# A hybrid decoder layer: the output projection of two token tiles at a time by one level of Strassen, and a re-paced second filter

## The chip, the cores and the metric

The kernel runs on one core of a Trainium2 chip. The core has five engines with their own instruction queues: TensorE (PE, matmuls), VectorE (DVE), ScalarE (ACT), GpSimd (POOL) and SyncE (SP, which here issues most DMAs). They share an on-chip memory (SBUF), in which the kernel's buffers lie; matmuls write to banks of a second memory (PSUM). The metric is the device time of one execution in microseconds, and the result of a version is the median of its runs.

## The reference

One decoder layer over 2048 tokens of width 1024, in float32, cut to what matters here:

```
hn     = rms_norm(h, mix_pre_g)
proj   = hn @ w_in                                  # q, k, v and the convolution's input u
attn   = sliding_window_attention(q, k, v, ...)     # window 128, 512 channels
conv   = conformer_conv(u, ...)                     # gate, 31-tap filter, LayerNorm, silu, pointwise; 512 channels
mixed  = concatenate([attn, conv]) @ w_out          # 1024 -> 1024: the output projection
h      = h + rms_norm(mixed, mix_post_g)
hn     = rms_norm(h, ffn_pre_g)
ff     = (silu(hn @ w_gate) * (hn @ w_up)) @ w_down # 1024 -> 2816 -> 1024
h      = h + rms_norm(ff, ffn_post_g)
```

Float32 products are made of three products each: both factors are split into a high part (a rounded copy) and a low part (the rest), and high·high, high·low and low·high are summed in PSUM (`three`, L167).

## The kernel before

**Tiles and stages.** The 2048 tokens are four tiles of 512. Letters name the stages, digits the tiles; in the profile a buffer's stage stands behind the "@". A is the input projection (`stage_a`), B the attention, whose result goes to rows 0 to 3 of a DRAM buffer `mixT`. T0 and T1 (`stage_taps`, L534) are the 31-tap filter of tile pairs 0/1 and 2/3: four channel groups of 50 VectorE operations each, shown under the label C. C (`stage_tail`, L586) is the rest of the convolution, LayerNorm and the pointwise product in the PSUM bank `ct`, and writes rows 4 to 7 of `mixT`. W (`stage_w`, L712) is the output projection; `norm_w` (L751) does what follows it for a tile: sum of squares, reciprocal root, scaling by `mix_post_g`, adding x, storing h, a second sum and root, and the scaled tile `hn`, which goes to `hn_scr` as well.

The FFN works on tile pairs and already uses one level of Strassen: H (`stage_h_plain` L833, `stage_h_sums` L846) reads `hn_scr` back, turns it on PE and makes plain operands and operand sums; F (`stage_pre` L891, then `stage_p1` L961) is the gate and up products; G (`stage_p2` L1119) the down product. H0, F0, G0 belong to tiles 0 and 1, H2, F2, G2 to tiles 2 and 3. `stage_pre` does those products of F that need plain operands only (20 matrices, two halves each of 12 matmuls, before the first p1, whose first product is the first to read a sum).

**The projection before.** `stage_w` works on one tile: eight chunks of 128 input channels, in groups of G = 2. `acts` loads a chunk of `mixT` into the raw buffer `mtag` and splits it (ScalarE the high part at L723, VectorE the low part); `weight` (L119) loads two weight chunks, and `split_w` (L108) makes the high part on ScalarE and the low part on POOL or, with `made`, loads a low part that an earlier tile left in `lo_out`. `block_half` (L686) does four token blocks of one half of the output columns: matmuls into a PSUM bank, then a copy (ScalarE, first group) or an addition (VectorE) into the tile's accumulator. That is 4 groups x 2 halves x 4 blocks x 6 matmuls = 192 a tile, 384 a pair.

**Order of the work.** Main work is a generator that `run` steps through; each step gives its cost, and by that cost lanes of side work earn credit (`Lane`, L1277) at a rate of their own: `lb` attention, `lc` filters, `lw` projections, `ld` tails, `lf`, `lh` FFN operands, `lt`. A lane's item may have a condition; `until` runs a lane through to a named item. The instructions then go to in-order queues, one an engine, in an order that a scheduler makes of it.

- W0 is an item of `lw`, once A3 has started and C0 is done. `lw.until("W0")` after A3 finishes it, its norm included; the H0 operands of tile 0 (B11.0, B21.0) become items of `lh`.
- W1 is main work, and with `ready` the first Q0 = 8 products of F0 run in its middle; its norm is given to `lh`. The sums S0 wait for product 22 of F0, B3 and T1.
- C2, W2, C3, W3 are items of `lw` beside G0 (`run(stage_p2((0, 1), ...))`), then N3 and B11.2; after G0, `lw.until("N3")` ends them, and F2 is main work.
- Raw chunks of W2 and W3, and the x that `norm_w` adds, use the tag `at`, of which there are two buffers.

Of the kernel before, what the change touches and what calls it, by code (L numbers as in the profile page):

```python
# [12 lines left out]
F32 = mybir.dt.float32  # L13
# [26 lines left out]
def layer_kernel(ctx, tc, x, xT, cols, rows, sinks, relb, onehot, w_in, w_pw, w_out, w_gate, w_up, w_down, out):  # L40
# [14 lines left out]
    BUFS = dict(x=4, p=4, wx=1, gb=2, hl=8, ql=4, chl=5, mid=4, mb=2, fa=4, at=2, fc=3, glu=1, yt=1, raw=2, w=6)  # L55
# [63 lines left out]
    def weight(src, low, made, raw=None, on_pool=True):  # L119
        if raw is None:  # L120
            raw = t_("raw", (P, 2, T))
            nc.sync.dma_start(raw, src)
        return [split_w(raw[:, n], "w", low[n], made, on_pool) for n in range(2)]
# [52 lines left out]
    lo_out = dr.tile([2, KC, P, T], F32, name="lo_out")  # L176
# [46 lines left out]
    kz = cst.tile([P, 2, P + T], F32R, name="kz")  # L223
    nc.gpsimd.memset(kz[:, :, 0:P].bitcast(F32), 0.0)
    junk = cst.tile([P, D], F8, name="junk")
    vtok = cst.tile([P, 5, P], F32, name="vtok")
# [307 lines left out]
    def stage_taps(p):  # L534
# [7 lines left out]
        for c in range(4):  # L542
# [14 lines left out]
            ay = t_("mb", (P, 2, T))  # L557
# [25 lines left out]
            nc.sync.dma_start(y_scr[c, :, p, 1], a)  # L583
            yield 0.0
# [101 lines left out]
    def block_half(acc, units, n, first, L, bank_of, s0=0):  # L686
        cs = slice(n * T, (n + 1) * T)
        for i in range(len(acc)):
            s = i + s0
            lab[0] = L  # L690
            o = bank_of()
            three(o, [((a[s // 4][:, 0, ss(s)], a[s // 4][:, 1, ss(s)]), (w[:, 0], w[:, 1])) for a, w in units])
            if first:
                act(acc[i][:, cs], o, AF.Copy)  # L694
            else:
                vtt(acc[i][:, cs], acc[i][:, cs], o, ALU.add)
            yield 0.65 * len(units)

# [13 lines left out]
    def stage_w(w, spill, G, atag, htag, mtag, bank_of, norm=None, ready=None):  # L712
        L = f"W{w}"
        lab[0] = L
        acc = [f4(atag) for _ in range(4)]

        def acts(gi):
            aa = []
            for c in range(G * gi, G * gi + G):
                m = f2(mtag)  # L720
                nc.sync.dma_start(m, mixT[c, :, w * T : (w + 1) * T])
                a = hl(htag)
                act(a[:, 0], m, AF.Copy)  # L723
                vtt(a[:, 1], m, a[:, 0].bitcast(F32), ALU.subtract)
                aa.append([a])
            return aa

        nxt = acts(0)
        for gi in range(KC // G):
            aa = nxt  # L730
            for n in range(2):
                lab[0] = L
                if n == 1 and gi + 1 < KC // G and not (ready and G * gi + G == 4):
                    nxt = acts(gi + 1)
                ws = weight(w_out[2 * gi : 2 * gi + 2, :, n * T : (n + 1) * T].rearrange("c p t -> p c t"),
                            lo_out[n, 2 * gi : 2 * gi + 2], w > 0)
                yield from block_half(acc, list(zip(aa, ws)), n, gi == 0, L, bank_of)
            if ready and G * gi + G == 4:
                for i, c in enumerate(ready()):
                    if i == Q0 // 2:  # L740
                        ld.until("C1")
                        lab[0] = L
                        nxt = acts(gi + 1)
                    yield c
        tail = norm_w(w, spill, acc, mtag)
        if norm:
            norm(tail)
        else:
            yield from tail

    def norm_w(w, spill, acc, mtag):  # L751
# [33 lines left out]
        for s in range(4):  # L785
            act(acc[s], acc[s], AF.Copy, scale=r2[:, s : s + 1])
            if spill:
                r0 = w * T + s * P
                nc.scalar.dma_start(hn_scr[r0 : r0 + P], acc[s])
# [291 lines left out]
    def stage_tsums(td):  # L1081
        L = "G0"
        for pr in range(NF // 2):
            lab[0] = L
            wx = f4("wx", (P, 2, T))
            b = [wx[:, 0], wx[:, 1], f2("fc"), f2("fc")]
# [235 lines left out]
    RC0, RC1, RW0, RW, RB, LC = 1.1, 0.9, 1.7, 1.25, 0.8, 100  # L1322
# [11 lines left out]
    Q0 = 8  # L1334
# [6 lines left out]
    lw = Lane(RW0, 0)  # L1341
# [4 lines left out]
    lanes = [lb, lc, lw, ld, lf, lh, lt]  # L1346
    lh.rates = {"N1": 1.2, "S0": 0.9, "H0": 1.2}
    lc.rates = {"T0": RC0, "T1": RC1}
    lw.rates = {"W0": RW0, "C2": RW, "W2": RW, "C3": RW, "W3": RW}
# [13 lines left out]
    lw.add("W0", stage_w(0, True, 2, "x", "hl", "fa", mm), lambda: "A3" in started and "C0" in ld.done)  # L1363
# [6 lines left out]
    for p in range(2):  # L1370
        lc.add(f"T{p}", stage_taps(p))
    for t in range(2):
        ld.add(f"C{t}", stage_tail(t), lambda: since(lc, "T0", CS))
    for t in range(NT):
# [33 lines left out]
    lw.until("W0")  # L1408
# [5 lines left out]
    for n, off in (("B11", 0), ("B21", 4)):  # L1414
        lh.add(n + ".0", stage_h_plain(ws, ops, n, off))
    run(stage_w(1, True, 2, "mid", "hl", "at", mm, norm=lambda g: lh.add("N1", g), ready=lambda: stage_pre(ws, ops, mids[0], keeps[0], 0, Q0)))
    lh.until("B21.0")
    lh.add("S0", stage_h_sums(ws, ops), lambda: f"P0.{PRE_S0}" in started and "B3" in lb.done and "T1" in lc.done)
    run(stage_pre(ws, ops, mids[0], keeps[0], Q0))
# [5 lines left out]
    lw.add("W2", stage_w(2, True, 2, "mid", "ql", "at", tr))  # L1425
# [74 lines left out]
```

## Time and profile before

| | us |
|---|---|
| median of 3 runs | 2112.7 |
| lowest and highest run | 2109.73 and 2113.94 |
| the profiled execution, its own time | 2107.25 |
| its span in the trace | 2105.5 |
| PE busy in the span | 1980.8 |
| VectorE busy in the span | 1448.8 |

The span runs from the first to the last recorded instruction; the rest of the execution's time lies around it. In the rows below, a group is a source line, an engine, an operation and "out<-in" with buffer names and stage letters, then partitions x elements, the count, busy microseconds, the mean of one in nanoseconds, and the idle time of the engine before them with what ended it. A timeline row gives the start in microseconds, the duration (of the whole run, where "x8" says that eight stand together), and in brackets the idle time before it with what ended it. A row of the DMA view ends with the size of one transfer and the median of the microseconds from issue to landing.

### The profile page before, as it was taken

How to read it: one execution, taken by the hardware profiler on the slowest of the kernel's cores; microseconds unless marked ns; L12 is line 12 of the kernel's file. 1: busy time of each engine (PE TensorE's matmuls, PEld its weight loads, DVE VectorE, ACT ScalarE, POOL GpSimd, SP SyncE). 2: the span in 40 equal slices, each digit the busy share in tenths (PEclk: the TensorE clock that was granted, in tenths of full speed). 3: DMA queues.
4: the chain of work that ended last, by engine and by line, in shares of the span. 5: the costliest groups of instructions: out<-in, count | busy, mean ns of one | idle time of the engine just before them, and what ended most of it. 6: DMA issues, size and time to landing. Idle time of an engine off the chain costs nothing. (4 is left out here: it accounts for less than half of the span.)

```text
span 2105.5 us, 27138 instructions
## 1 busy us (share of the span) xinstructions
PE 1980.8 (94%) x8826; PEld 1578.7 (75%) x8826; DVE 1448.8 (69%) x2530; ACT 990.4 (47%) x1938; POOL 410.7 (20%) x467
## 2 busy tenths in 40 slices
PE   9999997789797889999999999989999999999997
PEld 7777775467575667788877878878788888888886
DVE  4578999967799877767645465468476666446557
ACT  5455454436644653334336457356553343335443
POOL 4011022333311310000001103105333333220003
PEclk9999999799899999999999999999999999999999
DMA  8776645357665999854447678677964443266654
GB/s 312 259 267 225 206 160 166 119 167 257 221 196 186 331 319 310 278 170 168 147 155 245 212 227 292 209 258 265 338 212 167 170 166 124 91 220 228 194 191 148
DMA packets 237086, 451.32 MB, mean 214 GB/s; under 512 B 23400, under 2 KB 53264, under 8 KB 236944
## 3 DMA queue, kind: packets, MB, share of 16 engines
q1 hardware_dynamic: 216400, 419.18, 59.2%
q10 hardware_dynamic: 20544, 30.42, 3.9%
q8 instruction: 69, 1.13, 0.2%
q14 instruction: 73, 0.60, 0.1%
HBM read 330.48 MB, written 119.02 MB: 213 GB/s over the span
## 5 line engine op out<-in xcount | busy, mean ns | idle before, releaser
L888 PE MATMUL mm@F<-hl@H,w@F 128*128 128x512 f32 x1056 | 257.8, 395 | 9.4 <-ACT mm@F L928 9.4
L1158 PE MATMUL mm@G<-hl@G,hl@G 128*128 128x512 f32 x924 | 232.8, 399 | 10.8 <-ACT hl@G L801 4.6
L888 PEld LDWEIGHTS mm@F<-hl@H,w@F 128*128 128x128 f32 x1056 | 200.5, 191 | 53.6 <-ACT mm@F L928 11.7
L801 ACT ACTIVATE w@F<-chl@F 128x512 fp32r<-128x512 f32 x220 | 135.6, 625 | 166.1 <-PE mm@F L888 159.4
L1158 PEld LDWEIGHTS mm@G<-hl@G,hl@G 128*128 128x128 f32 x924 | 173.8, 191 | 51.2 <-ACT hl@G L801 5.4
L172 PE MATMUL mm@A<-hl@A,w@A 128*128 128x512 f32 x840 | 205.1, 395 | 5.2 <-DVE ql@A L87 2.1
L1158 PE MATMUL mm@G<-w@G,hl@G 128*128 128x512 f32 x876 | 199.4, 389 | 0.0
L1158 PEld LDWEIGHTS mm@G<-w@G,hl@G 128*128 128x128 f32 x876 | 164.4, 188 | 34.1
L87 DVE TENSOR_TENSOR w@F<-chl@F,w@F 128x512 fp32r<-128x512 f32 x198 | 146.2, 739 | 58.6 <-ACT w@F L801 58.1
L172 PEld LDWEIGHTS mm@A<-hl@A,w@A 128*128 128x128 f32 x840 | 154.9, 188 | 41.5 <-DVE ql@A L87 2.3
L888 PE MATMUL mm@F<-ql@H,w@F 128*128 128x512 f32 x528 | 131.5, 396 | 7.5 <-ACT mm@F L1035 4.7
L888 PE MATMUL mm@F<-x@H,w@F 128*128 128x512 f32 x528 | 127.6, 395 | 9.8 <-ACT fa@F L950 9.8
L888 PE MATMUL mm@F<-p@H,w@F 128*128 128x512 f32 x528 | 131.8, 395 | 0.0
L888 PE MATMUL mm@F<-mid@H,w@F 128*128 128x512 f32 x528 | 129.9, 392 | 1.8 <-DVE at@F L87 1.4
L888 PEld LDWEIGHTS mm@F<-x@H,w@F 128*128 128x128 f32 x528 | 100.2, 191 | 31.4 <-ACT fa@F L950 10.2
L888 PEld LDWEIGHTS mm@F<-ql@H,w@F 128*128 128x128 f32 x528 | 99.8, 190 | 31.2 <-ACT mm@F L1035 5.7
L112 ACT ACTIVATE w@A<-raw@A 128x512 fp32r<-128x512 f32 x110 | 67.6, 627 | 109.3 <-PE mm@A L172 75.7
L888 PEld LDWEIGHTS mm@F<-p@H,w@F 128*128 128x128 f32 x528 | 101.1, 192 | 21.6 <-ACT at@F L1049 0.2
L888 PEld LDWEIGHTS mm@F<-mid@H,w@F 128*128 128x128 f32 x528 | 98.5, 188 | 23.7 <-DVE at@F L87 1.8
L172 PE MATMUL mm@W<-w@W,hl@W 128*128 128x512 f32 x384 | 103.9, 418 | 10.6 <-ACT x@W L694 4.9
L87 DVE SCALAR_TENSOR_TENSOR mb@C<-wx@C,dws,mb@C 128x512 f32<-128x512 f32 x128 | 106.2, 830 | 1.8
L172 PE MATMUL tr@W<-w@W,ql@W 128*128 128x512 f32 x384 | 99.4, 397 | 6.7 <-ACT mid@W L694 4.8
(303 smaller groups left out, 3612.0 us busy)
## 6 DMA issues: line engine op xcount, KB each, us to landing
mids<-fa@F SPq DMA_DIRECT2D x154, 256.0 KB, 2.4
raw@A<-w_in SPq DMA_DIRECT2D x55, 512.0 KB, 4.4
w@A<-lo_in SPq DMA_DIRECT2D x84, 256.0 KB, 3.3
fc@G<-mids SPq DMA_DIRECT2D x77, 256.0 KB, 3.4
fa@G<-mids SPq DMA_DIRECT2D x75, 256.0 KB, 4.6
gb@F<-keeps SPq DMA_DIRECT2D x72, 256.0 KB, 4.3
raw@W<-w_out SPq DMA_DIRECT2D x32, 512.0 KB, 5.1
w@W<-lo_out SPq DMA_DIRECT2D x48, 256.0 KB, 3.5
```

What stands on the lines that cost most here:

```text
L87: r = op(*args, **kw)
L112: act(w[:, 0], raw, AF.Copy)
L172: mat(o, a, b, start=first and i == 0, stop=last and i == n - 1)
L801: act(w[:, 0], x, AF.Copy)
L888: mat(o, w[:, a, ks], op[k][:, b], start=first and n == 0, stop=n == 11, skip_group_check=not first)
L1158: mat(banks[b], p_, q_, start=start and z == 0, stop=stop and z == 2, skip_group_check=True)
```

## The change

`stage_w` now takes a pair of tiles and forms the product by seven half-size products (types 0 to 6) in place of eight. Type by type it does 4 token blocks of 12 matmuls: 7 x 4 x 12 = 336 a pair. Types 0 and 1 use tile one's channels 0 to 3 and 4 to 7 as they are, type 6 tile two's 4 to 7; types 2 to 5 use sums of the four. The first tile's accumulator is complete after type 4, the second's after type 6, and each is then handed with its norm to `on_tile`.

- `stage_wsums` (TW, lane `ld`, once A1 has started) makes four differences of weight quarters on POOL, 16 subtractions, into the DRAM buffer `tw`. `stage_wacts` (SA, lane `ld`) loads both tiles' `mixT` chunk by chunk, makes the four operand sums with 16 VectorE operations a pair, and stores them to `sa`, from where `acts` loads them.
- For the first pair `deep` loads and splits the next type's operands during the present one, and POOL makes all 28 low weight parts and leaves them in `lo_out`; the second pair loads them, and fetches a type's operands only after the type before.
- The first pair is main work after A3: `ld.until("SA")`, then `run(stage_w((0, 1), ...))`. N0, B11.0 and B21.0 go to `lh` after type 4, N1 after type 6. The eight products of F0 that ran inside W1 go back to the rest of F0 (Q0 is gone).
- S0 waits for "y11" (the second of T1's four channel groups stored) in place of the whole T1.
- Second pair in `lw`: C2, C3, SA2, W2; N2 goes to `lf`, N3 to `lw`, B11.2 waits for N2; `lw.until("W2")` after G0.
- Rates: filters RC0 1.1 to 1.4 and RC1 0.9 to 0.6; attention of tile 3 gets 0.55; W's 1.25 only.
- Buffers: T1's groups from the third on use `kz` in place of `mb`, and `stage_tsums` uses `vt` in place of `wx`, both former constants of their own.

```diff
-    lo_out = dr.tile([2, KC, P, T], F32, name="lo_out")
+    lo_out = dr.tile([7, 4, P, T], F32, name="lo_out")
+    tw = dr.tile([4, 4, P, T], F32, name="tw")
+    sa = [dr.tile([4, 4, P, T], F32, name=f"sa{i}") for i in range(2)]
...
-            ay = t_("mb", (P, 2, T))
+            ay = t_("kz" if p and c > 1 else "mb", (P, 2, T))
...
             nc.sync.dma_start(y_scr[c, :, p, 1], a)
+            started.add(f"y{p}{c}")
...
+    def stage_wsums():
+        for c in range(4):
+            y = t_("yt", (P, 4, T))
+            for i in range(4):
+                k, n = c + 4 * (i // 2), i % 2
+                nc.sync.dma_start(y[:, i], w_out[k, :, n * T : (n + 1) * T])
...
+            for to, o, p_, q_ in ((0, b11, b12, b11), (2, b12, b22, b12), (1, b22, b22, b11), (3, b21, b21, b22)):
+                ptt(o, p_, q_, ALU.subtract)
+                nc.sync.dma_start(tw[to, c], o)
...
+    def stage_wacts(ws):
+        for c in range(4):
+            r = [t_("chl", (P, 2, T)) for _ in range(2)]
...
+            vtt(s12[:, 0], r[1][:, 0], r[1][:, 1], ALU.add)
+            vtt(s12[:, 1], s12[:, 0], r[0][:, 0], ALU.subtract)
+            vtt(s34[:, 0], r[0][:, 0], r[1][:, 0], ALU.subtract)
+            vtt(s34[:, 1], r[0][:, 1], s12[:, 1], ALU.subtract)
+            nc.sync.dma_start(sc[0:2, c].rearrange("j p t -> p j t"), s12)
+            nc.sync.dma_start(sc[2:4, c].rearrange("j p t -> p j t"), s34)
...
+    def stage_w(ws, tags, htag, mtag, bank_of, deep, made, on_tile):
...
+        def evict(ty, b, o):
+            h = [x and (x[b][:, 0:T], x[b][:, T:]) for x in acc]
+            if ty == 0:
+                act(h[0][1], o, AF.Copy)
+            elif ty == 1:
+                vtt(h[0][0], h[0][1], o, ALU.add)
+            elif ty == 2:
+                vtt(h[1][0], h[0][1], o, ALU.add)
+            elif ty == 3:
+                act(h[1][1], o, AF.Copy)
+                vtt(h[0][1], h[1][0], o, ALU.add)
+            elif ty == 4:
+                vtt(h[0][1], h[0][1], o, ALU.add)
+            elif ty == 5:
+                vtt(h[1][0], h[1][0], o, ALU.add)
+                vtt(h[1][1], h[1][1], h[1][0], ALU.add)
+            else:
+                vtt(h[1][0], h[1][0], o, ALU.add)
...
+        aa, wt = acts(0, range(4)), weights(0, 0) + weights(0, 1)
+        for ty in range(7):
...
+            for b in range(4):
+                if deep and ty < 6:
+                    if b == 0:
+                        na += acts(ty + 1, (0, 1))
...
+                o = bank_of()
+                three(o, [((a[:, 0, ss(b)], a[:, 1, ss(b)]), (w[:, 0], w[:, 1])) for a, w in zip(aa, wt)])
+                evict(ty, b, o)
+                yield 2.72
...
+            if ty == 4:
+                on_tile(ws[0], norm_w(ws[0], acc[0], mtag))
+        on_tile(ws[1], norm_w(ws[1], acc[1], mtag))
...
-    RC0, RC1, RW0, RW, RB, LC = 1.1, 0.9, 1.7, 1.25, 0.8, 100
+    RC0, RC1, RW, RB, LC = 1.4, 0.6, 1.25, 0.8, 100
...
+    lb.rates = {"B3": 0.55}
...
-    lw.add("W0", stage_w(0, True, 2, "x", "hl", "fa", mm), lambda: "A3" in started and "C0" in ld.done)
...
+    ld.add("TW", stage_wsums(), lambda: "A1" in started)
...
+    ld.add("SA", stage_wacts((0, 1)), lambda: "B1" in lb.done)
...
-    run(stage_w(1, True, 2, "mid", "hl", "at", mm, norm=lambda g: lh.add("N1", g), ready=lambda: stage_pre(ws, ops, mids[0], keeps[0], 0, Q0)))
+    def on_first(w, norm):
+        lh.add(f"N{w}", norm)
+        if w == 0:
+            for n, off in (("B11", 0), ("B21", 4)):
+                lh.add(n + ".0", stage_h_plain(ws, ops, n, off))
+    ld.until("SA")
+    run(stage_w(ws, ("x", "mid"), "hl", "fa", mm, True, False, on_first))
...
-    lw.add("W2", stage_w(2, True, 2, "mid", "ql", "at", tr))
     lw.add("C3", stage_tail(3))
-    lw.add("W3", stage_w(3, True, 2, "mid", "ql", "at", tr, norm=lambda g: lw.add("N3", g)))
-    lw.add("B11.2", stage_h_plain(ws, ops, "B11", 0))
+    lw.add("SA2", stage_wacts(ws))
+    lw.add("W2", stage_w(ws, ("mid", "chl"), "ql", "at", tr, False, True, lambda w, norm: (lf if w == 2 else lw).add(f"N{w}", norm)))
+    lw.add("B11.2", stage_h_plain(ws, ops, "B11", 0), lambda: "N2" in lf.done)
     run(stage_p2((0, 1), mids[0], td))
+    lw.until("W2")
     lw.until("N3")
```

126 lines of the change are left out of this document (65 added, 61 removed).

## The prediction

> **What bounds the kernel now.** I read the page's totals first, then busy time by stretches cut at the places where TensorE (PE) passes from stage to stage, then the costs by group, and last the timeline around both places where the output projection (W) runs. The stretches:
>
> ```profile
> span 2105.5 us, 27138 instructions
> PE 1980.8 (94%) x8826; PEld 1578.7 (75%) x8826; DVE 1448.8 (69%) x2530; ACT 990.4 (47%) x1938; POOL 410.7 (20%) x467
> ...
> 0.00:200.00 200.00, 193.51 (x912) 150.97 (x912) 129.30 (x299) 100.79 (x217) 35.74 (x59) 1.00 0.76 268
> 200.00:420.00 220.00, 192.09 (x931) 140.25 (x929) 212.88 (x453) 97.80 (x260) 52.04 (x58) 0.93 0.52 166
> 420.00:525.00 105.00, 97.99 (x402) 71.47 (x403) 74.28 (x105) 50.49 (x87) 36.28 (x45) 0.92 0.63 210
> 525.00:775.00 250.00, 206.91 (x915) 157.72 (x914) 209.41 (x386) 132.30 (x272) 57.21 (x69) 0.92 0.74 251
> 775.00:1103.00 328.00, 319.25 (x1388) 261.62 (x1387) 217.50 (x344) 123.17 (x219) 0.00 (x0) 0.99 0.61 206
> 1103.00:1456.00 353.00, 337.18 (x1498) 274.27 (x1497) 209.15 (x357) 201.27 (x362) 60.82 (x96) 0.98 0.74 247
> 1456.00:2106.00 650.00, 633.90 (x2793) 522.46 (x2791) 396.25 (x589) 284.63 (x523) 168.64 (x141) 0.99 0.55 187
> ```
>
> After window and length the columns are busy time (and count) of PE, PEld, VectorE, ScalarE and POOL, then granted clock, DMA share, GB/s. PE bounds the whole at 94%, but not evenly. In the first 775 us it is busy 690.5 (the four rows added) and idle 84.5, with VectorE at 213 of 220 us in the second row. The last three rows have only 8.8, 15.8 and 16.1 us of PE idle. So removed matmuls are worth their full price after 775 us if nothing new stops PE; before 775 the filters and chains on VectorE decide.
>
> ```profile
> 1600.00:1650.00 50.00, 50.00 (x222) 41.42 (x221) 33.48 (x42) 19.26 (x35) 17.72 (x12) 1.00 0.51 173
> ...
> L172 PE MATMUL mm@W<-w@W,hl@W 128*128 128x512 f32 x384 | 103.9, 418 | 10.6 <-ACT x@W L694 4.9 <-ACT hl@W L723 4.3 <-DVE mid@W L87 1.3
> L172 PE MATMUL tr@W<-w@W,ql@W 128*128 128x512 f32 x384 | 99.4, 397 | 6.7 <-ACT mid@W L694 4.8 <-ACT ql@W L723 1.9
> ```
>
> An undisturbed stretch passes 222 matmuls in 50 us: **0.225 us each**. W is 384 matmuls for each pair of tiles (mm@W the first, tr@W the second), 203.3 us busy in all, with 17.3 us of waits of its own.
>
> **What is removed.** Seven products of four blocks of 12 matmuls are 336 a pair instead of 384: 48 x 0.225 = **-10.8 us per pair**, -21.6 in all. That is the most that the change can take out of PE. The stages not touched (p1 in the window from 775, and from 1456 to the end) I carry over at 327.5 and 649.
>
> **First part, up to p1.** Here W0 ran beside the last input projection, its norm and the H0 operands were ready while W1 ran, and PE had something to do meanwhile:
>
> ```profile
> 358.38 3.12 DVE L87 SCALAR_TENSOR_TENSOR mb@C<-wx@C,dws,mb@C 128x512 f32<-128x512 f32 x4
> 459.55 0.63 ACT L640 ACTIVATE fc@C<-ct@C 128x512 f32<-128x512 f32 x1 [1.63 <-PE ct@C L172]
> 466.21 0.60 ACT L527 ACTIVATE yt@C<-ct@C 128x512 f32<-128x512 f32 x1 [0.59 <-PE ct@C L526]
> 489.45 1.28 DVE L87 TENSOR_TENSOR x@W<-x@W,mm@W 128x512 f32<-128x512 f32 x2 [2.70 <-PE mm@W L172]
> 510.79 2.33 PE L172 MATMUL mm@A<-hl@A,w@A 128*128 128x512 f32 x9
> 541.72 1.13 ACT L786 ACTIVATE x@W<-x@W,sm@W 128x1024 f32<-128x1024 f32 x1
> 550.66 1.03 PE L819 MATMUL tr@H<-ident,fa@H 128*128 128x128 f32 x8
> 554.51 1.15 ACT L842 ACTIVATE x@H<-gb@H 128x512 fp32r<-128x512 f32 x2 [0.31 <-ACT chl@C L112]
> 572.43 0.64 ACT L640 ACTIVATE fc@C<-ct@C 128x512 f32<-128x512 f32 x1 [0.40 <-ACT gb@H L839]
> 587.73 2.88 PE L888 MATMUL mm@F<-x@H,w@F 128*128 128x512 f32 x12
> 775.16 1.52 PE L888 MATMUL mm@F<-mid@H,w@F 128*128 128x512 f32 x6
> ```
>
> The first filter pair ends at 361.5. The first tail (C0) ends at 460.2, 98.7 us later; C1 takes 466.2 to 573.1, 107 us. From W0's last addition (490.7) the norm runs to 542.9 (52 us), the transposes begin 7.8 us later, and the first operands are there at 555.7: **65 us from a tile's last addition to its first FFN operand.** W1 and the tails covered that.
>
> In the order of the changed program A3's last matmul is PE instruction 1,848 (2,097 before). The first two rows of the stretches count 1,843 PE instructions by 420 us, so A3 ends near **416** instead of 513. Only 72 W matmuls stand ahead of the second tail's work: products from the third on read the sums of mixT that the new SA pass makes out of both tails, and PE's next 175 instructions are only B3 and C1. Without W0 beside them I take 80 us for each tail, below the 98.7 and 107 shown: 361.5 + 160 = 521.5, and 18 us for the SA pass (four chunks, each loaded, added, stored and loaded again at 4.4 us a transfer, row below): W resumes near **540**. Bounds: 490 with tails of 60 us, 572 if C1 ends as it does now.
>
> From there 264 W matmuls remain, 59 us. The fifth product completes tile 0 after 168 of them: 540 + 38 = 578. Then the 65 us: 643. Products six and seven cover 21.6 us and PE runs out near 600, so some **35 us of idle appear** (less some B3 work). F0 begins near 642. Its 480 matmuls ahead of p1 cost 108 us at 0.225, and 137 at the rate of the stretch that holds them now:
>
> ```profile
> 700.00:750.00 50.00, 39.94 (x175) 32.37 (x176) 44.27 (x62) 33.61 (x61) 16.12 (x12) 0.93 0.98 336
> ...
> 750.28 1.75 DVE L87 TENSOR_TENSOR ql@H<-chl@H,ql@H 128x512 fp32r<-128x512 f32 x1
> ```
>
> That is 50/175 = 0.286 with the DMA engines at 0.98. The loads stay and the projection adds some, so I take 130, nearer the upper end: p1 begins near **772**, against 775, **-3**.
>
> A second path gives the same. p1 needs the operand sums, whose last operation ends at 752.0 on a VectorE that is busy 625.9 us up to 775. Ahead of that operation the changed order still has 198 of T1's 200 filter operations (200 before); the new gate on "y11" lets them start earlier, but the queue is no shorter. The pair itself has 72 VectorE operations in place of 64 (28 evictions, 28 splits, 16 sums against 48 and 16), +8 x 0.684. "Second filter spread" thus moves work and removes none: it takes cover from the first half and gives it to the second. If VectorE's idle time there falls by a third, 40 us, p1 begins at 740 (-35); if W resumes at 572 it begins near 800 (+25). These are the bounds.
>
> ```profile
> L87 DVE TENSOR_TENSOR mid@W<-mid@W,tr@W 128x512 f32<-128x512 f32 x48 | 32.1, 684 | 25.2 <-PE tr@W L172 25.2
> L114 POOL TENSOR_TENSOR w@W<-raw@W,w@W 128x512 fp32r<-128x512 f32 x16 | 23.1, 1447 | 66.1 <-ACT w@W L112 56.8 <-DMA raw@W<-w_out 9.2
> L87 DVE SCALAR_TENSOR_TENSOR x@W<-x@W,sm@W,gb@W 128x512 f32<-128x512 f32 x8 | 7.4, 997 | 1.2 <-POOL sm@W L141 1.2
> L87 DVE SCALAR_TENSOR_TENSOR mid@W<-mid@W,sm@W,gb@W 128x512 f32<-128x512 f32 x24 | 16.2, 745 | 8.8 <-DMA gb@W<-rows 5.0 <-POOL sm@W L141 3.8
> ```
>
> POOL gets 16 subtractions of weight quarters and 28 low parts instead of 16: 28 x 1.447 = 40.5 us. It is busy 181 of the first 775 us, so I cost this at nothing; uncovered, the 28 low parts alone pace W at 40.5 us against its 76 of matmuls, which still fits. The row x@W shows the same VectorE operation at 997 ns, mid@W at 745, with two SBUF inputs each. The Trainium skill (SBUF — State Buffer, "Who interferes with whom") says that a VectorE operation with two SBUF inputs and a POOL operation that reads SBUF hold one port pair in turn, each for its whole length, which speaks against giving POOL more work. By it the 28 additions could cost VectorE up to 40 us and p1 would begin later by as much; by the two rows, 252 ns a collision, 7 us. No run here separates the two yet.
>
> **Second part, beside G0.** Now tile 2's projection and norm end in the middle of G0, and tile 3's follow:
>
> ```profile
> 1233.19 1.52 PE L172 MATMUL tr@W<-w@W,ql@W 128*128 128x512 f32 x6
> 1234.75 0.69 DVE L87 TENSOR_TENSOR mid@W<-mid@W,tr@W 128x512 f32<-128x512 f32 x1 [0.90 <-PE tr@W L172]
> ...
> 1242.66 5.39 DVE L87 SCALAR_TENSOR_TENSOR mid@W<-mid@W,sm@W,gb@W 128x512 f32<-128x512 f32 x8 [2.32 <-POOL sm@W L141]
> ...
> 1257.61 0.69 DVE L87 TENSOR_TENSOR mid@W<-at@W,mid@W 128x512 f32<-128x512 f32 x1 [3.60 <-DMA at@W<-x]
> ...
> 1268.42 0.68 DVE L87 TENSOR_TENSOR mid@W<-at@W,mid@W 128x512 f32<-128x512 f32 x1
> ...
> 1282.93 1.13 ACT L786 ACTIVATE mid@W<-mid@W,sm@W 128x1024 f32<-128x1024 f32 x1
> ...
> 1452.66 2.49 PE L1158 MATMUL mm@G<-hl@G,hl@G 128*128 128x512 f32 x9 [0.49 <-DVE hl@G L87]
> 1456.22 5.96 PE L888 MATMUL mm@F<-ql@H,w@F 128*128 128x512 f32 x25
> ...
> at@W<-mixT SPq DMA_DIRECT2D x24, 256.0 KB, 4.4
> at@W<-x SPq DMA_DIRECT2D x14, 256.0 KB, 5.7
> ```
>
> The norm takes 1235.4 to 1284.1, **48.6 us**, all behind G0's matmuls; F2's first product starts 1.1 us after G0's last one ends (1455.2). In the changed order G0's last matmul comes first, and **144 W2 matmuls (products five to seven) and 20 transposes of H2 follow it with nothing of G0 between.** The fifth product completes tile 2, so its norm now starts after G0 has run out. On PE only products six and seven, 96 x 0.225 = 21.6 us, stand beside it.
>
> The seventh is late too. Its raw operands use the two "at" buffers and stand on SyncE's queue behind the norm's residual loads; ScalarE's split of its fourth chunk stands behind the norm's four scalings. So, counted from tile 2's last addition: scalings done at 48.6; the last split and its low part about 1.3; the rest of product seven 10.5; then the transposes (1.0 a row of four blocks) and copies and splits to the first operand 4 to 5: **F2 begins about 65 us after product five**, with 22 to 23 us of PE work in it: 42 us idle. If the gaps between residual additions (1251.6 to 1268.4, waiting for x) vanish, the norm takes 34 and the idle is 27.
>
> Stage from 1103 to 1456: 353.5 - 10.8 + 42, and +3 for product five, whose operands come one load and split after product four without prefetch, less 8 of its 15.8 us idle, as W's chunk waits (6.7, row tr@W) go with G0 work at hand: 379.7. I take the middle of 42 and 27 nearer the row as measured, 40: **+24**. Bounds +5 (norm of 34, all present idle gone) and +35 (nothing of it gone, seventh product fully behind).
>
> **The sum** against the profiled execution's own 2107.25 (span 2105.5 and 1.75 around it): -3 + 0 + 24 + 0 = +21, and 2128. The median shown, 2112.7, lies 5.5 above that execution; on its footing the forecast is 2112.7 + 21 = 2134, and I say **2132**.
>
> The row 420 to 525 grants 0.92 of the clock, the busy stretch at 1600 all of it. The Trainium skill (TensorE: Matmul & The Clock Gate, "Why this matters for your kernels") has the clock fall to half after about 3 us without matmuls, and a like time of work to restore it. By it the two new gaps would cost some 1.7 us each beyond their length, +3.4, as an estimate; the sum above leaves it out.
>
> **The rivals.**
> 1. *The gaps are covered* (faster). Norms of 34 us as bounded above, F0 drawn forward because VectorE is freed of W0 beside A3, and PE's 21.6 us come through: first part -25, second 0: 2088. For it: 17.5 us of the 48.6 are waits for x at a time when G0 shares every engine, and G0 will be gone. Against it: products six and seven put their loads, evictions and splits into the same queues, in the same two buffers.
> 2. *No net change.* One gap of about half my size and the saving cancel: 2112. Nothing in the profile prefers exactly this.
> 3. *The tails decide* (much slower). SA makes W wait for C1. If both tails run on VectorE beside T1 at today's 98.7 and 107 us, W resumes at 572, p1 begins at 800, and with +24 behind G0 the time is 2112.7 + 25 + 24 = 2162. It decides once C1 ends past 550. For it: both tails go through one PSUM bank, in line, and T1 and B3 share VectorE with them. Against it: W0's work left that stretch.
> 4. *The change does not do what it says*: the filter is not spread where it counts. That is already in my forecast (198 of 200).
>
> **How the numbers follow.** Forecast 0.45, with its own range 2116 to 2150; rival 1 0.28; rival 2 0.10; rival 3 0.17. What a measurement can tell from no change is about 4 us. Faster has rival 1, 0.28; same most of rival 2, 0.09; slower the rest, 0.63. The range 2092 to 2168 takes in rival 3 and rival 1's upper half.
>
> **What would show it.** PE without matmuls for over 30 us between W's seventh product and F0's first, and again between G0's last matmul and F2's first product: then both gap terms hold. C1's last row near 520 and W's resumption near 540 test the third number; p1's first product near 772 the first sum. I am wrong if F2 starts within 35 us of product five's last addition, if p1 starts before 745, or if PE's busy time in W falls by much less than 21.6 us at the full clock.

## The result and the profile after

The changed kernel takes 2218.49 us (median of four runs, 2212.13 to 2221.21); the kernel before took 2111.22 beside it. The ratio is 1.050 (95% interval 1.048 to 1.053): **107 us slower**, where 21 slower was forecast with a range up to 2168. The profiled execution has 2221.21, its span 2219.5.

The stretches of the changed kernel, cut again at PE's stages (columns as in the prediction: window, length, busy time and count of PE, PEld, VectorE, ScalarE, POOL, then granted clock, DMA share, GB/s):

```profile
span 2219.5 us, 27224 instructions
PE 1977.4 (89%) x8730; PEld 1571.1 (71%) x8730; DVE 1470.6 (66%) x2546; ACT 995.7 (45%) x1938; POOL 449.5 (20%) x495
...
0.00:200.00 200.00, 188.19 (x877) 145.97 (x878) 132.30 (x292) 97.67 (x213) 57.49 (x75) 0.97 0.87 300
200.00:421.00 221.00, 211.94 (x1040) 157.24 (x1039) 195.41 (x447) 102.08 (x269) 37.32 (x50) 0.98 0.58 181
421.00:545.00 124.00, 92.10 (x369) 58.23 (x367) 79.89 (x180) 53.07 (x136) 49.57 (x51) 0.74 0.35 108
545.00:694.00 149.00, 69.31 (x281) 55.77 (x282) 107.36 (x151) 46.65 (x79) 46.06 (x57) 0.73 0.67 220
694.00:832.00 138.00, 123.25 (x546) 97.93 (x546) 113.22 (x169) 80.99 (x142) 33.51 (x28) 0.96 0.87 298
832.00:1165.00 333.00, 320.69 (x1385) 262.02 (x1385) 224.88 (x357) 125.21 (x221) 0.00 (x0) 0.99 0.64 219
1165.00:1454.00 289.00, 282.45 (x1265) 230.83 (x1264) 156.03 (x254) 149.21 (x262) 28.44 (x40) 1.00 0.70 232
1454.00:1524.00 70.00, 42.87 (x163) 31.96 (x162) 31.38 (x54) 31.30 (x53) 10.85 (x27) 0.81 0.69 228
1524.00:1662.00 138.00, 103.33 (x428) 81.91 (x427) 92.45 (x143) 77.80 (x149) 59.21 (x61) 0.87 0.85 298
1662.00:2220.00 558.00, 543.31 (x2388) 449.26 (x2388) 337.72 (x504) 231.78 (x421) 127.04 (x109) 0.99 0.49 169
```

PE has the 96 matmuls fewer (8730 instead of 8826), which at 0.225 us each are 21.6 us, but its busy time falls by only 3.4 us. As an estimate, some 18 us are thus matmuls that ran longer. They lengthen where the granted clock is low (0.73 and 0.74 in the two stretches from 421 to 694); the 27 after the longest stop of the second pair, shown further down, take 8.17 us, 0.30 each. Three stretches hold most of the idle time: 421 to 694 (273 us, 111.6 idle), 1454 to 1524 (70, 27.1 idle) and 1524 to 1662 (138, 34.7 idle). Before, the last of these three, from F2's first product to p1, was this:

```profile
1456.00:1551.00 95.00, 92.23 (x404) 74.26 (x403) 62.10 (x93) 55.90 (x107) 42.82 (x34) 0.98 0.87 298
```

Place by place the 114 us between the two spans are: **start of F0's p1 831.6 instead of 775.2, +56; F0's p1 itself +6; from F0's end to F2's first product 358.7 instead of 353.5, +5; from there to F2's p1 138 instead of 95, +43; the rest +3.**

The timeline of the first place (start, duration, engine, line, operation; in brackets the idle time before it and what ended it):

```profile
544.48 0.62 ACT L643 ACTIVATE fc@C<-ct@C 128x512 f32<-128x512 f32 x1 [6.07 <-PE ct@C L172]
547.31 0.69 DVE L87 TENSOR_TENSOR chl@W<-chl@W 128x512 f32<-128x512 f32 x1 [33.52 <-DMA chl@W<-mixT]
553.85 0.69 DVE L87 TENSOR_TENSOR chl@W<-chl@W 128x512 f32<-128x512 f32 x1 [3.92 <-DMA chl@W<-mixT]
565.25 0.69 DVE L87 TENSOR_TENSOR chl@W<-chl@W 128x512 f32<-128x512 f32 x1 [5.78 <-DMA chl@W<-mixT]
574.16 0.69 DVE L87 TENSOR_TENSOR chl@W<-chl@W 128x512 f32<-128x512 f32 x1 [5.69 <-DMA chl@W<-mixT]
576.89 3.36 PE L172 MATMUL mm@W<-chl@W,hl@W 128*128 128x512 f32 x7 [32.45 <-ACT chl@W L112]
...
631.76 0.67 DVE L87 TENSOR_TENSOR x@A<-x@A,mm@W 128x512 f32<-128x512 f32 x1
682.82 1.13 ACT L856 ACTIVATE x@A<-x@A,sm@W 128x1024 f32<-128x1024 f32 x1
690.43 1.11 PE L888 MATMUL tr@H<-ident,fa@H 128*128 128x128 f32 x4 [43.56 <-DMA fa@H<-hn_scr]
693.75 1.79 PE L957 MATMUL mm@F<-x@H,w@F 128*128 128x512 f32 x4
...
831.58 1.64 PE L957 MATMUL mm@F<-ql@H,w@F 128*128 128x512 f32 x3 [2.21 <-ACT mm@F L1104]
```

C1, the second tail, ends at 545.1. The four rounds of SA's additions then run one after another, the last beginning at 574.2: a round is 6.5 to 11.4 us. PE is empty for 32.4 us, finishes the second half of product two, and starts product three at 585.3. Product two reads no sum; its second half waits for its weights (`chl@W`, written at L112), which lie in the five `chl` buffers that SA's rounds hold. VectorE stands still for 33.5 us with these additions at the head of its queue. Tile 0's norm takes from its last addition (632.4) to 684.0, 51.5 us; PE is empty for 43.6 us ahead of H0.

And around G0's end and F2's first part:

```profile
1451.80 1.52 PE L1226 MATMUL mm@G<-hl@G,hl@G 128*128 128x512 f32 x6
...
1466.18 0.68 DVE L87 TENSOR_TENSOR mid@G<-mid@G,tr@W 128x512 f32<-128x512 f32 x1
...
1500.88 8.17 PE L172 MATMUL tr@W<-w@W,ql@W 128*128 128x512 f32 x27 [16.10 <-ACT ql@W L755]
...
1509.72 1.13 ACT L856 ACTIVATE mid@G<-mid@G,sm@W 128x1024 f32<-128x1024 f32 x1
1510.76 0.61 ACT L755 ACTIVATE ql@W<-at@W 128x512 fp32r<-128x512 f32 x1
...
1523.65 34.04 PE L957 MATMUL mm@F<-ql@H,w@F 128*128 128x512 f32 x146
...
1590.50 5.49 PE L957 MATMUL mm@F<-mid@H,w@F 128*128 128x512 f32 x12 [17.86 <-ACT mm@F L997]
...
1662.11 0.73 PE L957 MATMUL mm@F<-hl@H,w@F 128*128 128x512 f32 x2 [0.95 <-ACT w@F L870]
```

The accumulators carry names of earlier stages (x@A, mid@G) because they reuse those buffers. Product seven waits 16.1 us for its raw operands, and ScalarE's split of its fourth chunk (1510.76) stands right behind the norm's last scaling (1509.72), as the order said it would. F2's first part then stops again, 17.9 us at once, and its p1 begins 138 us after it began. What ends that stop is a copy on ScalarE (L997), which is busy for 17.35 of the 18 us from 1572 to 1590: the last scalings of tile 3's norm, copies of B21, and sums of squares of G0's own result (L1171). Sixteen of these sums ran between 1418.9 and 1476.5 before; now they stand behind tile 3's norm in the queue and run from 1563.7 to 1589.9.

### The profile page after: what moved, and what is told of

Its sections match the earlier page's. It is cut to its first block, busy times and chain, and to the rows that moved or that the text cites. A ratio compares the mean times of both kernels' runs of the same rounds, so it can differ in the third digit from the quotient of the medians.

```text
span 2219.5 us, 27224 instructions
## 1 busy us (share of the span) xinstructions
PE 1977.4 (89%) x8730; PEld 1571.1 (71%) x8730; DVE 1470.6 (66%) x2546; ACT 995.7 (45%) x1938; POOL 449.5 (20%) x495
## 5 line engine op out<-in xcount | busy, mean ns | idle before, releaser
L1226 PE MATMUL mm@G<-hl@G,hl@G 128*128 128x512 f32 x924 | 223.5, 392 | 4.5 <-DVE hl@G L87 2.4
L957 PE MATMUL mm@F<-mid@H,w@F 128*128 128x512 f32 x528 | 139.7, 412 | 32.9 <-ACT mm@F L997 28.5
L957 PEld LDWEIGHTS mm@F<-mid@H,w@F 128*128 128x128 f32 x528 | 104.8, 200 | 58.5 <-ACT mm@F L997 30.5
L172 PE MATMUL tr@W<-w@W,ql@W 128*128 128x512 f32 x336 | 90.2, 409 | 26.8 <-ACT ql@W L755 25.6
L112 ACT ACTIVATE w@A<-raw@A 128x512 fp32r<-128x512 f32 x110 | 67.1, 626 | 90.5 <-PE mm@A L172 65.7
L484 POOL TENSOR_SCALAR_AFFINE_SELECT p@B<-p@B 128x512 f32<-128x512 f32 x62 | 51.5, 840 | 238.7 <-ACT p@B L482 237.3
L87 DVE TENSOR_TENSOR w@G<-raw@G,w@G 128x512 fp32r<-128x512 f32 x73 | 52.3, 716 | 68.6 <-ACT w@G L870 67.4
```

The costliest lines, as they stand in the source:

```text
L87: r = op(*args, **kw)
L112: act(w[:, 0], raw, AF.Copy)
L172: mat(o, a, b, start=first and i == 0, stop=last and i == n - 1)
L484: nc.gpsimd.affine_select(out=pg[:, kb].rearrange("p (i q) -> p i q", q=P), in_=pg[:, 1].rearrange("p (i q) -> p i q", q=P), compare_op=AL ...
L957: mat(o, w[:, a, ks], op[k][:, b], start=first and n == 0, stop=n == 11, skip_group_check=not first)
L1226: mat(banks[b], p_, q_, start=start and z == 0, stop=stop and z == 2, skip_group_check=True)
```

## The experiments

Where no number of runs is given, a time is that of a single run. Thirteen runs of the kernel before in one session spread from 2106.25 to 2121.83, so differences of a few microseconds between single runs say little; places in a trace say more.

**One half of the change at a time.** First the first pair joint and tiles 2 and 3 one by one as before, except that POOL makes tile 2's low weight parts, which the kernel before loads:

```diff
...
     lw.add("C2", stage_tail(2))
+    lw.add("W2", stage_w1(2, True, 2, "mid", "ql", "at", tr))
     lw.add("C3", stage_tail(3))
-    lw.add("SA2", stage_wacts(ws))
...
+    lw.add("W3", stage_w1(3, True, 2, "mid", "ql", "at", tr, norm=lambda g: lw.add("N3", g)))
...
```

> First pair joint as changed, second pair one tile at a time as before. Theory: the loss has two independent places, about +56 us ahead of F0's p1 and about +49 us between G0 and F2's p1 (5 in the G0 stretch, 43 in F2's first part), because the joint pair completes its second tile last and its norm then has only 384 matmuls in front of it. Then this kernel keeps only the first: about 2215 - 49 = 2166 (2158 to 2175), F2's p1 about 95 us after F2's first product instead of 138. Rival (the loss behind G0 is only the first one's delay passed on, VectorE or DMA being late): above 2195.

Measured: 2164.64 us; p1 of F0 at 832.2, F2's p1 100 us after F2's first product. So the +49 around G0's end belong to the second pair, and the first place stays as it was. The agreement of the whole hides one thing: from F0's end to F2's first product this kernel takes 343.0 us, 10 less than the kernel before (353.4), for a reason that no run isolates.

Then the reverse, the kernel before with only the second pair joint (the old `stage_w` and the old pacing for the first; POOL makes the second pair's low parts):

> First pair one tile at a time with the pacing of before, second pair joint (its 28 low parts made on POOL). Theory of two independent places: about 2110 + 49 = 2159 (2150 to 2170), p1 of F0 at about 775 again. Rival (second place only a consequence of the first): within 15 us of before.

Measured: 2180.99, 22 more than expected. F2's p1 comes 137 us after F2's first product, as in the changed kernel, so the two places are independent. But p1 of F0 is at 791.7, not 775, with nothing changed ahead of it but the 16 weight differences (TW). They were meant for after A1's start, and run from 28.9 to 97.1 us: the scheduler put them where POOL was free. The busy time of the first 200 us, in this kernel and in a later one whose differences are made during F0's p1 (the last version below):

```profile
0.00:200.00 200.00, 188.60 (x878) 146.48 (x878) 133.81 (x292) 97.96 (x213) 57.13 (x75) 0.97 0.88 300
```

```profile
0.00:200.00 200.00, 193.41 (x905) 151.81 (x907) 127.79 (x296) 100.05 (x216) 35.05 (x59) 0.99 0.78 266
```

PE gets 27 instructions fewer done by 200 us, with the DMA engines at 0.88 instead of 0.78; p1 differs by 14 us (791.7 against 777.7). The count holds over the traces kept: 870 to 884 in the thirteen kernels with early differences, 898 to 912 in the three without. The price at p1 is from one run each, so it is rough, and the subtractions on POOL are moved together with their transfers. The rest of this kernel's excess lies beside G0 (1113.9 to 1485.4, 371.6 us for 358.6 in the changed kernel), where POOL makes the low parts that the changed kernel loads; no run shows that this is the cause.

**The sums of the first pair on POOL.** Is it VectorE, blocked by the additions, that makes p1 late?

```diff
-            vtt(s12[:, 0], r[1][:, 0], r[1][:, 1], ALU.add)
...
+            add = vtt if ws[0] else ptt
+            add(s12[:, 0], r[1][:, 0], r[1][:, 1], ALU.add)
...
```

> As changed, but the 16 operand sums of the first pair run on POOL instead of VectorE. Theory V: the sums wait at the head of VectorE's queue for the second tail (33.5 us, then 5.8 and 5.7) while ready filter operations stand behind them, and p1 waits for VectorE; on POOL the filter goes on, and p1 starts 30 to 50 us before 831 although W itself resumes up to 10 us later: about 2180. Theory P: p1 is set by the chain on PE (W resumes, norm of tile 0, 480 matmuls of F0); W resumes 5 to 10 us later and the time is 2218 to 2230.

Measured: 2228.75, p1 at 839.9. The number is theory P's, but the trace says that the test did not free VectorE:

```profile
561.06 1.01 DVE L87 TENSOR_TENSOR hl@W<-fa@W,hl@W 128x512 fp32r<-128x512 f32 x1 [46.11 <-ACT hl@W L756]
```

The next instruction in VectorE's order, the split of product three's operands, waited for the same sums, 46.1 us long. A block at the head of an in-order queue passed to the next instruction that needs the same data. The question stayed open.

**The old pacing** (filters 1.1 and 0.9, tile 3's attention at the common rate, sums after the whole second filter):

> As changed, but with the old pacing: filters at 1.1 and 0.9, attention of tile 3 at the common rate, operand sums after the whole second filter. Theory V: more of the second filter stands ahead of the blocked additions, so p1 starts 10 to 30 us earlier: 2185 to 2208. Theory P: the tails come later on VectorE, W resumes later, p1 within 10 us or later: 2208 to 2235.

Measured: 2220.58; VectorE finishes the second filter at 774 instead of 828 and the sums at 818.1 instead of 822.4, but p1 begins at 843.9, 12 us later: theory P's case. F0's p1 itself then takes 326.3 us instead of 333.4, which makes up for half. The other way round, **the new pacing alone on the kernel before**:

> The kernel before with the pacing of the change alone (filters 1.4 and 0.6, attention of tile 3 at 0.55, operand sums once two channel groups of the second filter are stored, its last two groups in 'kz'). My forecast took the spread as neutral. If the second filter's operations only move, within 5 us of before (2107 to 2118). Rival: slowing the second filter delays the operand sums and p1 (which stand behind it on VectorE): 8 to 25 us slower.

Measured over ten runs: 2111.62 against 2115.25, ratio 0.998 (0.996 to 1.000). The spread is neutral in both kernels as far as the whole time goes. It does move work: F0's p1 takes 334.4 us here and 327.7 in the kernel before, so the +6 of that stage in the changed kernel goes with the pacing.

**Taking waits for the norms away.** F0's plain operands read from x in place of tile 0's normalised result:

```diff
-        nc.sync.dma_start(t, hn_scr[w * T : (w + 1) * T, k * P : (k + 1) * P].rearrange("(s p) c -> p s c", p=P))
+        nc.sync.dma_start(t, (hn_scr if w else x)[w * T : (w + 1) * T, k * P : (k + 1) * P].rearrange("(s p) c -> p s c", p=P))
```

> As changed, but F0's plain operands are turned from x instead of tile 0's normalised result, so they wait for no norm (the output differs from the reference). Theory P (W's end, then the norm of tile 0 with nothing on PE, then 480 matmuls of F0): the 43.6 us gap between W's last matmul and F0's first shrinks below 10, F0 begins near 655, and p1 comes 25 to 40 us earlier (792 to 806): about 2185. Theory V (p1 waits for the operand sums, which stand behind the second filter on VectorE): F0 begins earlier as well, but waits again ahead of p1; p1 at 820 or later, 2205 to 2220.

Measured: 2203.43, F0's first product at 684.0, p1 at 819.3. The dependence was gone and most of the gap stayed, so the time fell short of theory P by 18 us and lies just below theory V's range, for a reason that neither names:

```profile
660.04 1.11 PE L888 MATMUL tr@H<-ident,fa@H 128*128 128x128 f32 x4 [16.34 <-DMA fa@H<-x]
...
684.04 2.50 PE L957 MATMUL mm@F<-x@H,w@F 128*128 128x512 f32 x5 [11.53 <-ACT x@H L911]
```

The transposes came 30 us earlier than in the changed kernel, but ScalarE's copies and splits of H0 stand in its queue among the norm's own steps (its scalings begin at 678.2), so the operand waited for the norm all the same. The same for F2's sums, turned from tile 2 in place of tile 3 (`b12 = turned(2, ...)`, `b22 = turned(2, ...)`):

> As changed, but F2's operand sums are turned from tile 2's normalised result in place of tile 3's, so they wait for no second norm (the output differs from the reference). If F2's p1 is late because the norm of tile 3 now stands behind the whole projection, p1 follows F2's first product by 95 to 110 us instead of 138 and the time is 2180 to 2192. Rival: the sums are slow for DMA (share 0.97 in that stretch) or for buffers and queues that the second norm still holds; p1 still 125 us or more after F2's first product, above 2205.

Measured: 2228.43, F2's p1 142.5 us after its first product: no gain, as the rival said. And tile 2's second operands (B21) in buffers of their own and not held for N3:

> As changed, but tile 2's second set of plain operands (B21) loads its columns into 'fc' instead of sharing the two 'at' buffers with the x loads of tile 3's norm, and is not held back for that norm. If B21 behind these buffers makes the 17.9 us stop in F2's first part, that stop goes, but p1 still waits for the sums: p1 5 to 15 us earlier, 2203 to 2213. Rival (the norm of tile 3 and the sums alone set p1): p1 within 4 us, the time 2214 to 2222.

Measured: 2229.45, p1 145 us after F2's first product: a miss for both theories' numbers, no gain. But the 17.9 us stop did go, as the first theory said, and another came at p1 itself:

```profile
1671.11 4.50 PE L957 MATMUL mm@F<-hl@H,w@F 128*128 128x512 f32 x9 [22.18 <-ACT w@F L870]
```

The last operation on the operand sums ends at 1668.7 on VectorE, the first weight sums of p1 stand right behind it there, and ScalarE's copy of them releases PE. Two chains thus end close together, B21 and the sums. This run and the one before it each took one away; no run took both.

**The norms taken out as work.** Tiles 0, 2 and 3 store their accumulators and skip everything else in `norm_w`:

```diff
+        if w != 1:
+            for s in range(4):
...
+                nc.sync.dma_start(h_scr[r0 : r0 + P], acc[s])
+                nc.scalar.dma_start(hn_scr[r0 : r0 + P], acc[s])
...
+            return
```

> As changed, but the norms of tiles 0, 2 and 3 are left out altogether (no sums of squares, no roots, no scaling, no x loads and additions; their accumulators go straight to h_scr and hn_scr). Theory N: these chains, now behind the projection with little on PE beside them, make all three stops. Then F0's first product follows product five of the first pair by 20 to 30 us instead of 71 and p1 of F0 comes 20 to 40 us earlier; F2's first product follows G0's last matmul by about 36 us (144 matmuls) instead of 70; p1 of F2 follows F2's first product by 90 to 110 us instead of 138. In all 2105 to 2150. Rival: p1 stays late after F0's and F2's first products for the transfers and splits of the sums themselves (138 both times, DMA share 0.97): 2155 to 2185.

Measured: **2139.13, 79 us of the 107 gone.** Its stretches from C1 to F0's first product, on to p1, and at F2:

```profile
541.00:658.00 117.00, 72.15 (x297) 56.45 (x298) 86.82 (x120) 34.96 (x60) 23.79 (x16) 0.81 0.81 270
658.00:789.00 131.00, 120.26 (x530) 96.43 (x528) 119.85 (x180) 78.50 (x138) 36.17 (x40) 0.95 0.90 304
...
1416.00:1485.00 69.00, 47.22 (x174) 34.05 (x172) 37.02 (x69) 21.86 (x45) 9.31 (x7) 0.85 0.87 305
1485.00:1584.00 99.00, 94.86 (x430) 77.86 (x431) 50.27 (x62) 61.14 (x111) 36.50 (x26) 0.98 0.88 294
```

F0 begins at 657.9 instead of 693.8 (37 us after product five, not the 20 to 30 expected), p1 at 789.3 instead of 831.6 (42 us), and F2's first part takes 98.5 us instead of 138 (40 us). The third place, expected at 36, did not move: 69.7 us from G0's last matmul to F2's first product, against 70.3. There product six waits 9.6 us and seven 2.6 and 1.3 for raw operands, with the DMA engines at 0.87. Counted from product five's last matmul, F2 begins 48.4 us after it instead of 57.9, so the norm's absence counts there, and what is won is lost on the way to product five. This fits a second pair whose own loads, fetched one type at a time, are nearly as late as the norm; no run took both away. The norms' work is gone here, not only its place, so 79 us bounds from above what their place costs. The kernel before was not run without the same norms, so the share of the work itself is open.

**The serial pass over mixT.** The raw chunks of SA in the free `mid` buffers:

```diff
-            r = [t_("chl", (P, 2, T)) for _ in range(2)]
+            r = [t_("chl" if ws[0] else "mid", (P, 2, T)) for _ in range(2)]
```

> As changed, but the first pair's sums read their raw chunks into the free 'mid' buffers, so chunks do not queue for five 'chl' buffers. If the four chunk rounds (about 9.5 us each after the second tail) are serial because of the buffers, W's third product begins near 568 instead of 585 and the whole gains 12 to 20 us: 2198 to 2207. Rival: the rounds are serial because loads and stores queue on SyncE behind each other's waits; then W resumes within 5 us of 585 and the time is 2213 to 2223.

Measured: 2213.73 (median of two runs, the profiled one 2211.66). Product three starts at 567.2 instead of 585.3, 18 us earlier, as the first theory said; half of it is lost again by p1 (822.7, 9 us earlier), and the whole time is the rival's: its 5 us below 2218.49 are within the spread of runs. The rounds are not all side by side either: they begin at 541.0, 543.6, 552.7 and 561.4, the last two still waiting for their own loads. Beside the missing norms:

> As changed, but without the norms of tiles 0, 2 and 3 and with the raw chunks of the first pair's sums in the free 'mid' buffers. If the two effects add (2139 without norms; 18 us earlier resumption, about 9 us at p1 with the buffers), p1 at about 775 to 782 and 2125 to 2133. If nothing but the norms' place costs time at p1, within 4 us of 2139.

Measured: 2122.84, p1 at 782.2. The two add up (p1 is 7 us earlier than without the norms alone), and leave some 15 us to the kernel before in the same session (2107.69).

**Less of the second filter**, to tell PE's chain from VectorE's load:

> As changed, but the second filter pair runs with 2 of its 15 steps of each subfilter and 3 of its 16 last ones, about 160 of 200 operations (some 120 us of VectorE) less, its result wrong. Theory P (W resumes, norm of tile 0, 480 products of F0): p1 within 10 us of 831, as W's third product, F0's first product and the pace of 480 products do not depend on the filter; 2205 to 2222. Theory V (VectorE's load): p1 30 us or more earlier, because the norm, the weight splits of F0 and the sums come through sooner; F0's 480 products take about 115 us instead of 138; 2170 to 2190.

Measured: 2191.87, p1 at 798.9. Neither theory has it whole. W's third product starts at 582.3 (585.3), so the filter does not hold W back. F0's 480 matmuls take 133.5 us (138), so their pace is not VectorE's load either. But F0's first product comes at 665.3, 28 us earlier: product five's last addition ends at 616.0 instead of 632.4, and the norm behind it takes 39.8 us instead of 51.5, both through a shorter queue. That p1 is 33 us earlier is theory V's number, by way of the norm alone. **p1 is set by PE's chain, and the filter's operations, queued among the norm's steps on VectorE, make the norm's link of that chain longer.**

**The differences later** (the gate on TW moved from A1 to A3):

> As changed, but the weight differences (16 POOL subtractions, 4 MB read and 4 MB written) start with A3 instead of A1. In the changed kernel A1 ends 10 us later than before, A2 9 us. If the differences' DMAs and POOL operations cause that, A2 ends near 298 instead of 307, A3 near 414 instead of 421, and 3 to 9 us remain of it at the end: 2209 to 2216. Rival (the delay comes from elsewhere or is absorbed later): within 3 us of 2218.

Measured: 2230.88 over two runs, slower. The edit did not do what it was for: the differences still ran from 27 to 95 us, since the gate only orders the program text; the order of A3 and C0 changed, and C1 ended at 558.8 instead of 545.1.

**A version without the wait for two tails.** Seven products within one tile (its two halves of 256 tokens), tile 2 only, on the kernel before:

> The kernel before, with tile 2 alone projected by seven products over its own two halves of 256 tokens (168 matmuls in place of 192; its weight differences made in p1, where POOL is idle), so it needs its own tail only. If the saving is worth 0.225 us a matmul where nothing new waits, and tile 3's projection still ends over 45 us ahead of F2, 5 us faster than before (2103 to 2110). Rival: tile 2's longer chain of loads pushes tile 3's norm behind G0 (75 us of cover become 49): 5 to 25 us slower.

Measured over seven runs: 2128.2 against 2113.77, ratio 1.006 (1.004 to 1.008). Products three to seven of tile 2 run from 1232.9 to 1283.5, and W3 ends at 1403.6 instead of 1373.5; F2's p1 comes 109 us after its first product instead of 95, which fits the rival: a norm pushed towards F2. That is 14 of the 16 us between the two spans. The differences, now made during F0's p1, come with 8 us more there (335.7 for 327.7), and the stretch from F0's end to F2's first product gives 8.5 back (344.9). No version tried beats the kernel before by more than the spread of runs.

## Why the prediction was wrong, step by step

- **"The stages not touched ... I carry over at 327.5 and 649"**: the step that failed worst. From F2's first product to the end is 695.9, +47, and 43 of it lie ahead of p1. The forecast followed tile 2's norm to F2's first product and stopped there. Tile 3's projection now ends at 1517.1 instead of 1373.5, so its norm, B21 and the operand sums all fall into F2's first part, which before held only the second half of the sums (B21's transposes ended at 1427.8, half of the sums' at 1456.2). Without the norms that part is back at 98.5 us. F2's instructions were untouched; what had to be ready for them was not.
- **"W resumes near 540"**, with its bound of 572: it is 585.3. A3's end is near the forecast (421 against 416), partly by luck: the trace has A3's last matmul as PE instruction 1,914, not 1,848, and PE was faster there than in the rows of before. Tails of 80 us gave 521.5, C1 ended at 545.1; and "18 us for the SA pass" is 40. The four rounds were costed as one round of transfers, as if they overlapped, and at 4.4 us from a row of 256 KB; the pass moves 512 KB in 6.1 us in and 6.6 out. With five shared `chl` buffers the rounds ran one after another, and free buffers took 18 us off.
- **The norm of tile 0**: 65 us were forecast from the last addition to the first operand; the trace has 632.4 to 693.4, 61. The idle gap is 43.6 us for "some 35". The mechanism held. What was missed is that the last addition itself came 9 us after product five's last matmul (623.0 to 631.8), behind other work on VectorE.
- **F0's 480 matmuls**: 130 forecast, 138 measured. Together: 45 at W's resumption, 7 to F0's first product, 8 to p1, which are the 60 between 772 and 831.6. The first part was forecast at -3 and came out at +56, so the forecast's right direction, slower, rests on the second part alone and is partly luck.
- **"I cost this at nothing"** for POOL: PE never waited for a low part of the first pair, but the early differences did not hide. They run beside A0 with the DMA engines at 0.88 instead of 0.78, and two kernels that differ ahead of p1 in them alone are 14 us apart there. The traces bear out the prediction's sentence on the port pair: of the 28 splits of operands that VectorE makes while POOL makes the first pair's low parts, 20 take 0.69 us and 8 take 0.95 to 1.78, and just these 8 overlap a POOL operation of over 1 us. Where the second pair's low parts are loaded, all 28 are short; where POOL makes them (the kernel above with only the second pair joint), 9 are long.

```profile
L87 DVE TENSOR_TENSOR hl@W<-fa@W,hl@W 128x512 fp32r<-128x512 f32 x28 | 26.8, 966 | 13.6 <-ACT hl@W L755 13.5
L87 DVE TENSOR_TENSOR ql@W<-at@W,ql@W 128x512 fp32r<-128x512 f32 x28 | 19.3, 690 | 44.1 <-ACT ql@W L755 44.0
```

The price is 7.8 us of VectorE, near the 7 forecast, not 40. The 252 ns behind that 7 were a mean over operations hit and spared: a hit costs up to 1.1 us.
- **+24 beside G0**: +5 measured. The terms of the lower bound, +5 there, add up to +3. G0's last matmul comes with 6.5 us of idle behind it since 1165, less than the 15.8 before; then F2 begins 57 us after tile 2's last addition, for 65 forecast, with 27.1 us of idle for 42. The queue order behind the seventh product was read rightly. That the norm alone makes this gap was not shown: counted from G0's last matmul it was as long with the norms gone. The sign asked for, PE without matmuls for over 30 us, did not come here (27.1 us in pieces, 16.1 the longest); at the first place it did (43.6).
- **"Second filter spread" moves work and removes none**: right, 0.998 by itself. In the lower bound beside it, "a third, 40 us" does not match its row: VectorE is idle for 149 of the first 775 us, and a third is 50.
- Of the rivals, "the tails decide" named the right place in the first part with too low a price (572 as W's latest resumption), though its own condition, C1 past 550, was not met: C1 ended at 545.1, and what came late was the pass behind it. The one mechanism that cost most after F2's start was on no list.
- The clock: the stretches with gaps show it at 0.73 and 0.81 granted. In the 43.6 us gap it is 0.50 from 655 to 690, still 0.50 until 694 with matmuls back, and 1.00 from 700. This agrees with the prediction's sentence on the clock gate. That sentence's +3.4 counted two gaps; the 18 us of longer matmuls estimated above come from all stops, and no run separates the clock's share.

Open: what the remaining 15 us are made of beyond the early differences, and how F2's first part divides between tile 3's norm, B21, the sums and G0's own sums of squares. In-order queues fit what was seen when the sums used tile 2's data; an order written with the sums ahead of N3 was not tried.

## What to carry to other kernels

When an algorithm saves work by joining two tiles, look first at when its two results complete: here both come at the end, so two norm chains of 50 us lost the matmuls that covered them, for 21.6 us saved. Follow such a chain to the last consumer, past stages whose own code is unchanged. Taking away a data dependence proves little where in-order queues keep the old order; taking the work itself out answers the question.

## What the runs showed of the hardware that was not expected

- A wait on an in-order engine is handed on. With the additions on POOL, VectorE's 33.5 us stop became one of 46.1 us at the next instruction that needed the sums. With the wait for tile 0's norm gone, ScalarE still brought the operand only 10 us earlier.
- Work that nothing waits for soon still cost: with 16 early differences (4 MB read, 4 MB written, and their subtractions on POOL) the DMA share of the first 200 us was 0.88 instead of 0.78, and PE got 27 instructions fewer done. Whether the transfers or the subtractions cost this was not separated.
- Beside POOL's low parts, 8 of 28 VectorE operations with two inputs in SBUF took 0.95 to 1.78 us instead of 0.69, 7.8 us in all; where POOL had none to make, 28 of 28 took 0.69.
- Half of an 18 us gain at one link (567.2 against 585.3) was gone at the end of the same chain (822.7 against 831.6).
